# Regrouping the last output pairs, the last norm's steps, a look-ahead of weights and the low parts of the pooling in a one-core decoder step

## The chip, the cores and the metric

The kernel runs on one core of one Trainium2 chip. The time is device microseconds (us) of one launch; the kernel before takes 2322.99 us, the median of three runs (2320.79 to 2325.85). Engines are named as in the profile: PE is TensorE (PEld its weight loads), DVE is VectorE, ACT is ScalarE, POOL is GpSimd, SP is SyncE, whose queue issues most DMAs.

## The reference

One inference step of a decoder with two layers, width 2048, in fp32. There are 1024 prompt tokens and 8 sampled tokens that each continue a sequence of their own. In outline, prompt and samples alike:

```
z = x @ w_in_a;  u, gate = z[:, :2048], z[:, 2048:]
d = mean of u over the last 2, 4, 8, 16 tokens (four groups of 512 channels) - u
d = per-group linear(d) * scale
h = layer_norm(ALPHA * x + (d * silu(gate)) @ w_out_a)          # layer A
k, v = h @ w_kv                                                  # 4 heads of 64, rotary on k
q, gate = h @ w_in_b                                             # 32 heads of 64
o = attention over the last 128 tokens, with a learned sink per head
y = layer_norm(ALPHA * h + (o * silu(gate)) @ w_out_b)          # layer B
```

The outputs are y for prompt and samples, and the new pooling states, keys and values.

## The kernel before, in words

**Stages.** The tokens are cut into two chunks, c = 0 (512 tokens) and c = 1 (512 tokens and the 8 samples, 520 columns). PHASES runs the input side of layer A (ai0, ai1), its output side (ao0, ao1), the input side of layer B with the attention (bi0, bi1) and its output side (bo0, bo1). Everything is transposed: channels lie on the partitions, tokens on the free axis.

**Products.** A 2048x2048 block is multiplied by Strassen's scheme: for each pair of 128-row output tiles `seven()` makes seven products, in the order ORDER7. Every fp32 operand is split into a high part (rounded to the format that PE multiplies) and a low part (the rest), so a product is 8 row blocks times 3 matmuls (L684 to L686): 24 matmuls of 128x128 by 256 or 260 columns. Behind a product stand its posts, which take the results out of PSUM: copies on ACT (L623 p0, L632 and L657 p5 and p6, L629, L638, L644, L647) and additions on DVE (L645, L650; L636 and L655 in the last pairs).

**Weights ahead.** `begin()` (L531) runs ahead of each product. With `self.ahead = a, b, d` it issues the loads (L285, 512 KB each, on the SP queue) up to a products ahead, the high parts (L505, ACT) up to b ahead and the low parts (L520, DVE) up to d ahead. The value is 7, 4, 3 in Strassen stages, and 6, 4, 3 from the end of bi1 until 23 products into bo0. In bi1 it falls to at most 6, 3, 2 whenever fewer than three whole buffers are free. Inputs of a product (high and low part of combined x tiles, L828 loads, L838 ACT, L847 DVE) are made ahead in the same way by `x_tick`.

**Memory and order.** There are 54 buffers of 128 x 1040 floats; the one that has been free longest is taken. PE, DVE and ACT run in the order of the source (`in_order`). The SP queue issues in order too: a load whose buffer is still in use holds back everything behind it.

**From bi0 to bi1.** The last two pairs of bi0 make queries and gates of chunk 0, `queries(p)` (L2148) calls `x_begin(nxt)` at the last one, and bi1 begins with the shared keys and values: weights `in_wkv`, and input sums of h (`h1`, `th1`). Between them run the attention of chunk 0 (L1874 scores, L1923 and L1910 exponentials, L1936, L1963 store of o by POOL) and rotary's partner rows, fetched by four DMAs (L1728).

**Pooling in ai0 and ai1.** For each tile `pool_tail` (L1106) finishes the mean (L1131 subtracts u); a step later `rest()` makes the high part on ACT; `low()` makes the low part on DVE (L1150) and frees the buffers. With c = 1 low() follows at once, with c = 0 another step later.

**Norm of chunk 0 during bo1.** `ln_gen` (L1066 on) yields between steps; `end()` (L544), at the end of each product, takes a step when self.every (2.75 in bo1) products have passed and enough buffers are free. For a pair it loads the raw output (L994), subtracts the mean (L1068), multiplies by 1/sigma (L1069), applies gain and bias on ACT (L1060) and stores (L1061).

**The end, phase_end.** bo1's chunk is cut into columns A (the first 260, prompt tokens) and Bh (260 more). The last pairs, SPLIT = 5, 6, 7, called x, y, z, make their 21 products in turns, in the order TAIL; `steps` says which helper runs ahead of which product: x_in (load of the residual), less (ALPHA*h minus a shift), rest (adds the residual), square (ACT), add (accumulates sums and squares, DVE), stats (mean and 1/sigma of Bh), affine1 (L1474, L1478: subtract mean, multiply, DVE), affine2 (ACT L1485 twice, and the out_y store L1486), back (reloads an earlier pair), scale (gain, ACT) and spare (POOL). After the last product stand the last square and sums, `moments` (L1545, mean and 1/sigma of A), POOL's four steps on the last four columns (L1619 to L1622), `last_rows` (L1594: rank-one matmuls that finish the transposed rows of A) and `evict` (L1602), which scales 8 PSUM banks of 128x512 into four tiles, each stored to y1a with one DMA of 512 KB.

Of the kernel before, what the change touches and what calls it, by code (L numbers as in the profile page):

```python
# [66 lines left out]
SPLIT = 5, 6, 7  # L67
TAIL = (
    (5, 0), (5, 2), (5, 1), (6, 0), (5, 3), (5, 4), (6, 2), (6, 1), (7, 0), (6, 3), (7, 2), (7, 1), (6, 4),
    (7, 3), (7, 4), (5, 5), (5, 6), (6, 5), (6, 6), (7, 5), (7, 6),  # L70
# [120 lines left out]
class Kern:  # L191
# [789 lines left out]
    def ln_gen(self, c, pre, acc, gc, bc, out, td):  # L981
# [81 lines left out]
        for p in range(10):  # L1063
            load(p + 2)
            if p < 8:
                t = self.pair_view(pre[p], T)  # L1066
                if c == 0:
                    nc.vector.tensor_sub(t, t, b2(mu))  # L1068
                nc.vector.tensor_mul(t, t, b2(rr))  # L1069
# [52 lines left out]
    def pool_tail(self, c, i, g, w, U, s, T, ext, dd, bufs, Us, work, add):  # L1122
# [20 lines left out]
        def rest():  # L1143
# [10 lines left out]
            low() if c else self.at(1, low)  # L1154
# [249 lines left out]
    def phase_end(self, c, xs, x_in, pre, acc, gc, bc, out):  # L1404
# [30 lines left out]

        def square(p, h, j=slice(0, 2)):
            if p not in q:
                q[p] = self.mem.full(2 * T)
            nc.scalar.activation(self.pair_view(q[p], T)[:, j, h], tv(p)[:, j, h], AF.Square)

        def add(p, h):
            nc.vector.tensor_add(av[:, :, h], av[:, :, h], tv(p)[:, :, h])
            nc.vector.tensor_add(qv[:, :, h], qv[:, :, h], self.pair_view(q[p], T)[:, :, h])

        def sums(h):
# [3 lines left out]
            for ps, a, w in zip(R[h.start], (av, qv), (tv(z), self.pair_view(q[z], T))):  # L1449
                srcs = [v[:, j, h] for v in (a, w) for j in range(2)]  # L1450
# [3 lines left out]
        def stats(h):  # L1454
# [4 lines left out]
            nc.scalar.copy(m, mb[:, :TH])  # L1459
            nc.vector.tensor_mul(qq, m, m)  # L1460
# [76 lines left out]
        def sums_z(n):  # L1537

            w = (tv(z), self.pair_view(q[z], T))[n]
            for j in range(2):  # L1540
                nc.tensor.matmul(
                    R[0][n][:, :TH], J, w[:, j, A], start=False, stop=j == 1, skip_group_check=True,
                )

        def moments():  # L1545
# [15 lines left out]
            affine1a(1, Bh)  # L1561
# [7 lines left out]
            affine1b(1, Bh)  # L1569
# [32 lines left out]
        def evict(b, k):  # L1602
# [3 lines left out]
            r = box["rc"][:, b : b + 1]  # L1606
            if k % 2:
                nc.vector.tensor_scalar(y, X[b, k][:], r, None, op0=ALU.mult)  # L1608
# [3 lines left out]
            else:  # L1612
                nc.scalar.activation(y, X[b, k][:], AF.Copy, scale=r)
# [13 lines left out]
        x, y, z = SPLIT  # L1627
        for p in SPLIT:
            box, z0, z1 = self.two(T)

            def open_(p=p, box=box, z0=z0):
# [6 lines left out]
            (x, 0): [lambda: x_in(y)],  # L1638
            (x, 2): [lambda: less(x)],
            (y, 0): [lambda: x_in(z)],  # L1640
# [8 lines left out]
            (z, 3): [lambda: rest(y, Bh), lambda: square(y, Bh), lambda: back(1), lambda: back(2)],  # L1649
            (z, 4): [  # L1650
                lambda: add(y, Bh), lambda: rest(y, A), lambda: back(3), lambda: back(4),
                lambda: spare(0), lambda: scale(0),
            ],
# [13 lines left out]
        }  # L1667
        for p, idx in TAIL:
            for go in steps.get((p, idx), []):
                self.at(0, go)  # L1670
            if (p, idx) == (x, 5):
# [13 lines left out]
        scale(y)  # L1685
        spare(y)
        spare(z)
        affine1(z, Bh)
# [793 lines left out]
```

## Time and profile before

| | |
|---|---|
| Runs | 2322.99 us median, 2320.79 to 2325.85 |
| Profiled execution | 2320.17 us, span 2317.9 us (2.27 us lie outside the span) |
| Granted TensorE clock, mean | 0.997 |
| PE busy | 2288.1 us, 99% of the span |
| DVE busy | 1943.0 us, 84% |
| ACT busy | 1389.3 us, 60% |
| POOL busy | 191.1 us, 8% |
| DMA | 649.37 MB, mean 280 GB/s |
| Largest stall of PE inside the program | 4.92 us, at 1506.68 to 1511.60 us |
| Last matmul product ends | 2296.1 us after the start of the span |

Times inside the trace count from the start of the span. A row of the list of instructions gives the start, the time from start to end, engine, line, operation, output and inputs, a count, and in brackets how long the engine had been idle before it and what ended that. Rows of SPq are DMA issues. A row of the waits gives total us, times, and the longest one. A matmul is shown 0.28 us long although the next begins 0.12 us later, since they are pipelined.

### The profile page before, as it was taken

What the parts mean: (1) busy time and instruction counts of PE and PEld (TensorE: products, weight loads), DVE (VectorE), ACT (ScalarE), POOL (GpSimd) and SP (SyncE); (2) the same over time, 40 slices, a digit from 0 to 9 for tenths busy, and PEclk for the clock granted to TensorE, in tenths of its full rate; (3) what the DMA queues carried; (4) which work ended last, traced back from release to release, by engine and by line L of the source; (5) the groups of instructions that cost most, each with busy time, mean ns of one, the idle gap of its engine ahead of it and who ended that gap; (6) DMA issues with size and microseconds to landing.
All of it is one profiled execution on the core that took longest, in us unless ns stands there. A gap on an engine that the chain in (4) does not pass through costs nothing. (4 is left out here: it accounts for less than half of the span.)

```text
span 2317.9 us, 50529 instructions
## 1 busy us (share of the span) xinstructions
PE 2288.1 (99%) x20417; PEld 2217.7 (96%) x20417; DVE 1943.0 (84%) x2409; ACT 1389.3 (60%) x2548; POOL 191.1 (8%) x360
## 2 busy tenths in 40 slices
PE   9999999999999999999999999999999999999997
PEld 7999999999999999999889999989999999999997
DVE  8888889877878878988979898889877777889797
ACT  5544446544546547655566767685776678556565
POOL 0111110010000000000001111100000000000001
PEclk9999999999999999999999999999999999999999
DMA  7869679999989989999767666777787878799795
GB/s 261 287 242 315 229 245 330 315 309 303 304 302 322 335 284 333 317 392 345 245 234 241 233 234 236 252 259 250 234 252 240 252 230 288 251 360 381 252 330 184
DMA packets 246682, 649.37 MB, mean 280 GB/s; under 512 B 25232, under 2 KB 106032, under 8 KB 246448
## 3 DMA queue, kind: packets, MB, share of 16 engines
q1 hardware_dynamic: 204432, 493.66, 63.8%
q0 software_dynamic: 42016, 152.49, 17.0%
q8 instruction: 159, 2.61, 0.5%
q14 instruction: 75, 0.61, 0.1%
HBM read 463.54 MB, written 173.01 MB: 275 GB/s over the span
## 5 line engine op out<-in xcount | busy, mean ns | idle before, releaser
L684 PE MATMUL pD<-m,m 128*128 128x260 f32 (+1 forms) x5088 | 1441.3, 283 | 4.7 <-ACT pD L623 2.3
L686 PE MATMUL pD<-m,m 128*128 128x260 f32 (+1 forms) x5088 | 1434.7, 282 | 4.9 <-DVE m L520 4.9
L685 PE MATMUL pD<-m,m 128*128 128x260 f32 (+1 forms) x5088 | 1434.7, 282 | 0.0
L684 PEld LDWEIGHTS pD<-m,m 128*128 128x128 f32 x5088 | 959.4, 189 | 13.9 <-issue 6.2
L686 PEld LDWEIGHTS pD<-m,m 128*128 128x128 f32 x5088 | 959.8, 189 | 7.1 <-DVE m L520 7.0
L685 PEld LDWEIGHTS pD<-m,m 128*128 128x128 f32 x5088 | 959.1, 189 | 0.5
L520 DVE TENSOR_TENSOR m<-m,m 128x1024 fp32r<-128x1024 f32 x690 | 833.5, 1218 | 94.7 <-ACT m L505 44.1
L505 ACT CAST m<-m 128x1024 fp32r<-128x1024 f32 x690 | 720.5, 1049 | 249.9 <-DVE m L349 120.3
L349 DVE TENSOR_TENSOR m<-m,m 128x1024 f32<-128x1024 f32 x136 | 166.1, 1222 | 10.2 <-DMA m<-in_wia 5.7
L847 DVE TENSOR_TENSOR m<-m,m 128x1024 fp32r<-128x1024 f32 (+1 forms) x118 | 143.8, 1224 | 7.4 <-ACT m L838 5.8
L838 ACT CAST m<-m 128x1024 fp32r<-128x1024 f32 (+1 forms) x118 | 123.3, 1051 | 11.8 <-DVE m L520 3.5
L657 ACT COPY m<-pD 128x260 f32<-128x260 f32 (+1 forms) x89 | 33.2, 373 | 131.0 <-PE pD L686 131.0
L645 DVE TENSOR_TENSOR m<-pD,m 128x260 f32<-128x260 f32 (+1 forms) x92 | 38.4, 418 | 73.1 <-ACT pD L644 67.2
L1910 ACT ACTIVATE m<-m,sm 128x128 f32<-128x128 f32 x256 | 99.4, 392 | 0.0
L623 ACT ACTIVATE pD<-pD 128x260 f32<-128x260 f32 (+1 forms) x90 | 33.3, 370 | 102.2 <-PE pD L686 102.0
L1179 PE MATMUL pD<-m,m 128*128 128x260 f32 (+1 forms) x528 | 91.5, 323 | 0.0
L712 PE MATMUL pD<-m,m 128*128 128x512 f32 x224 | 89.1, 398 | 0.0
L714 PE MATMUL pD<-m,m 128*128 128x512 f32 x224 | 88.2, 394 | 0.0
L713 PE MATMUL pD<-m,m 128*128 128x512 f32 x224 | 88.1, 393 | 0.0
L1179 PEld LDWEIGHTS pD<-m,m 128*128 128x128 f32 x528 | 79.4, 188 | 8.2
L1923 ACT ACTIVATE m<-m,sm 128x128 f32<-128x128 f32 x256 | 81.8, 391 | 3.8 <-DVE sm L1918 3.4
L632 ACT COPY m<-pD 128x260 f32<-128x260 f32 (+1 forms) x92 | 34.3, 373 | 82.3 <-PE pD L686 82.0
(257 smaller groups left out, 2101.3 us busy)
## 6 DMA issues: line engine op xcount, KB each, us to landing
m<-in_wib SPq DMA_DIRECT2D x132, 512.0 KB
m<-in_wia SPq DMA_DIRECT2D x128, 512.0 KB
m<-swoa SPq DMA_DIRECT2D x64, 512.0 KB
swia<-m POOLq DMA_DIRECT2D x56, 512.0 KB, 4.9
m<-swia SPq DMA_DIRECT2D x56, 512.0 KB
m<-swob SPq DMA_DIRECT2D x56, 512.0 KB
m<-in_wob SPq DMA_DIRECT2D x52, 512.0 KB
m<-in_woa SPq DMA_DIRECT2D x48, 512.0 KB
```

Of the source, the lines that this page charges most:

```text
L349: self.nc.vector.tensor_add(s[out].a[:, :1024], s[x].a[:, :1024], s[y].a[:, :1024])
L505: self.nc.scalar.copy(hi.r[:, :1024], self.stream[self.cast].src().a[:, :1024])
L520: self.nc.vector.tensor_sub(lo.r[:, :1024], s.src().a[:, :1024], hi.a[:, :1024])
L684: nc.tensor.matmul(ps[:, :TH], wh[:, s], h, start=new and k == 0, stop=False, skip_group_check=on)
L685: nc.tensor.matmul(ps[:, :TH], wh[:, s], l, start=False, stop=False, skip_group_check=on)
L686: nc.tensor.matmul(ps[:, :TH], wl[:, s], h, start=False, stop=k == 7, skip_group_check=on)
L712: nc.tensor.matmul(ps[:], wh[:, s], h, start=par == 0 and k == 0, stop=False)
L714: nc.tensor.matmul(ps[:], wl[:, s], h, start=False, stop=par == 1 and k == 7)
L838: self.nc.scalar.copy(h.r[:, :n], s.a[:, :n])
L847: self.nc.vector.tensor_sub(l.r[:, :n], s.a[:, :n], h.a[:, :n])
L1179: nc.tensor.matmul(ps[:, : cs.stop - cs.start], ws[:, s], d[:, cs], start=f0 and k == 0, stop=l0 and k == 3,)
L1910: nc.scalar.activation(x["s3"][:, i, :], x["s3"][:, i, :], AF.Exp, bias=nm[:, i : i + 1], scale=0.125, accum_out=rs[:, i : i + 1],)
```

## The change

Four edits.

1. **The end.** SPLIT becomes 4, 5, 6, 7, called w, x, y, z: four pairs are made in turns, 28 products, with pair 4's last two products near the end. Squares take a half buffer each and free it in add. Every affine1 but that of y and z moves ahead of the last product, and so does affine2 of pairs 0, w, 1, 2 and x; pair 3 alone gets its affine2 later. Pair 4 needs no store and reload. Of the scale and spare steps, those of y move ahead of the last product. The evictions no longer alternate with affines, and five of the eight run on DVE, three on ACT (before, four and four).
2. **The norm of chunk 0 in bo1.** A yield stands between subtraction and multiplication when the result is the final output, and self.every falls from 2.75 to 1.5.
3. **Pooling.** low() follows at once for means over 8 and 16 tokens, and a step later for those over 2 and 4, in both chunks. So chunk 0's wide groups make it earlier, chunk 1's narrow ones later.
4. **bi0 to bi1.** From the last query pair of bi0, loads run 8 products ahead instead of 7, for 30 products: the 14 left of bi0 and 16 of bi1.

```diff
-SPLIT = 5, 6, 7
+SPLIT = 4, 5, 6, 7
...
                 if c == 0:
                     nc.vector.tensor_sub(t, t, b2(mu))
+                    if td is None:
+                        yield
                 nc.vector.tensor_mul(t, t, b2(rr))
...
-            low() if c else self.at(1, low)
+            low() if w > 4 else self.at(1, low)
...
-                q[p] = self.mem.full(2 * T)
+                q[p, h.start] = self.mem.half(T)
...
+            q.pop((p, h.start)).free()
...
             nc.scalar.copy(m, mb[:, :TH])
+            rest(z, A)
             nc.vector.tensor_mul(qq, m, m)
...
-            affine1a(1, Bh)
+            affine1a(z, Bh)
...
-            (x, 6): [
-                lambda: stats(Bh), lambda: spare(1), lambda: scale(1), lambda: spare(2), lambda: scale(2),
-            ],
-            (y, 5): [
-                lambda: square(x, A), lambda: affine(0, Bh), lambda: spare(3), lambda: scale(3),
-            ],
-            (y, 6): [
-                lambda: add(x, A), lambda: rest(z, A), lambda: spare(x), lambda: scale(x),
-            ],
-            (z, 5): [lambda: square(y, A), lambda: affine(x, Bh), lambda: spare(4), lambda: scale(4)],
+            (w, 6): [lambda: stats(Bh), lambda: spare(1), lambda: scale(1)],
+            (x, 5): [lambda: square(w, A), lambda: affine(0, Bh), lambda: spare(2), lambda: scale(2)],
+            (x, 6): [lambda: add(w, A), lambda: spare(w), lambda: scale(w)],
+            (y, 5): [lambda: square(x, A), lambda: affine(w, Bh), lambda: spare(3), lambda: scale(3)],
+            (y, 6): [lambda: add(x, A), lambda: affine(1, Bh), lambda: spare(x), lambda: scale(x)],
+            (z, 5): [lambda: square(y, A), lambda: affine(2, Bh), lambda: affine1(x, Bh)],
             (z, 6): [
-                lambda: square(z, A, 0), lambda: add(y, A), lambda: scale(z, (0,), True),
+                lambda: square(z, A, 0), lambda: add(y, A), lambda: scale(z, (0,), True), lambda: scale(y),
+                lambda: spare(y), lambda: affine1(3, Bh), lambda: affine2(x, Bh),
             ],
...
         affine1(y, Bh)
         scale(z, (1,))
-        scale(y)
-        spare(y)
         spare(z)
-        affine1(z, Bh)
...
-            affine2(z, Bh)
+            affine2(3, Bh)
         last_rows(0, range(4))
         last_rows(1, range(3))
-        affine1(2, Bh)
-        for k in range(4):
-            evict(0, k)
-        last_four()
-        affine2(1, Bh)
+        evict(0, 0, False)
+        evict(0, 1, True)
+        evict(0, 2, True)
+        affine2(z, Bh)
         X[1, 3] = self.psD()
         turn(1, 12, 16)
         last_rows(1, (3,))
-        affine1(3, Bh)
-        affine2(2, Bh)
-        for k in range(4):
-            evict(1, k)
-        affine1(4, Bh)
-        affine2(3, Bh)
-        affine2(4, Bh)
+        evict(0, 3, True)
+        last_four()
+        evict(1, 0, False)
+        evict(1, 1, True)
+        evict(1, 2, False)
+        evict(1, 3, True)
...
                 if c == 1:
                     self.ahead = 6, 4, 3
+                else:
+                    self.ahead = 8, 4, 3
+                    self.at(30, lambda: setattr(self, "ahead", (7, 4, 3)))
...
-                self.every, self.room = 2.75, 3
+                self.every, self.room = 1.5, 3
```

The SP queue at the turn from bi0 to bi1, before (in_wkv is the weight of keys and values, h and th the inputs of bi1's sums, L1728 the partner rows):

```order
L285 DMA m_1974_17956<-in_wib 128x1024
L828 DMA m_1979_18002<-h_95 128x4x260
L828 DMA m_1989_18088<-th_92 128x4x260
L1728 DMA m_1977_17995<-m_1962_17784 32x1024 x4
L828 DMA m_1978_18000<-h_95 128x4x260
L285 DMA m_1980_18006<-in_wkv 128x1024
L828 DMA m_1983_18044<-h_95 128x4x260
L828 DMA m_1984_18046<-h_95 128x4x260
L285 DMA m_1986_18050<-in_wkv 128x1024
L285 DMA m_1990_18091<-in_wkv 128x1024
```

The same place with the change (L1732 is the old L1728):

```order
L285 DMA m_1975_17958<-in_wkv 128x1024
L285 DMA m_1970_17912<-in_wib 128x1024
L828 DMA m_1979_18002<-h_95 128x4x260
L1732 DMA m_1978_17997<-m_1963_17786 32x1024 x4
L828 DMA m_1980_18004<-h_95 128x4x260
L285 DMA m_1981_18008<-in_wkv 128x1024
L828 DMA m_1984_18046<-h_95 128x4x260
L828 DMA m_1985_18048<-h_95 128x4x260
L285 DMA m_1987_18052<-in_wkv 128x1024
L828 DMA m_1990_18090<-th_92 128x4x260
```

The first load of in_wkv moves ahead of the inputs and of the partner rows, the second comes directly behind the partner rows and one input, and the load of th that stood ahead of the partner rows now stands behind the third load of in_wkv.

DVE around the end of the last product, before: L636 and L655 take z's last two products from PSUM, and then come four affines of two rows each before L1557, the first row of `moments`.

```order
L1442 TENSOR_TENSOR m_2839_26557<-m_2839_26557,m_3008_27968 128x2x260
L1443 TENSOR_TENSOR m_2921_27166<-m_2921_27166,m_3045_28331 128x2x260
L655 TENSOR_TENSOR m_3025_28141<-pD_28576,m_3025_28141 128x260
L1474 TENSOR_TENSOR m_3008_27968<-m_3008_27968,m_3058_28452 128x2x260
L1478 TENSOR_TENSOR m_3008_27968<-m_3008_27968,m_3058_28452 128x2x260
L1474 TENSOR_TENSOR m_3025_28141<-m_3025_28141,m_3058_28452 128x2x260
L1478 TENSOR_TENSOR m_3025_28141<-m_3025_28141,m_3058_28452 128x2x260
L1557 TENSOR_TENSOR m_3067_28650<-m_3066_28649 128x260
```

With the change (L1447, L1448 are the old L1442, L1443; L1481, L1485 the old L1474, L1478; L1564 the old L1557):

```order
L636 TENSOR_TENSOR m_3022_28091<-pD_28561,m_3022_28091 128x260
L1447 TENSOR_TENSOR m_2842_26560<-m_2842_26560,m_3004_27917 128x2x260
L1448 TENSOR_TENSOR m_2926_27183<-m_2926_27183,m_3048_28320 128x2x260
L1481 TENSOR_TENSOR m_3047_28313<-m_3047_28313,m_3055_28395 128x2x260
L1485 TENSOR_TENSOR m_3047_28313<-m_3047_28313,m_3055_28395 128x2x260
L655 TENSOR_TENSOR m_3022_28091<-pD_28595,m_3022_28091 128x260
L1481 TENSOR_TENSOR m_3004_27917<-m_3004_27917,m_3055_28395 128x2x260
L1485 TENSOR_TENSOR m_3004_27917<-m_3004_27917,m_3055_28395 128x2x260
L1564 TENSOR_TENSOR m_3069_28672<-m_3065_28620 128x260
```

One affine less stands between L655 and the moments, and one more ahead of L655.

The last stores of the SP queue, before (y1c are the four last columns, y1a the rows of A, out_y the columns Bh of a pair):

```order
L1623 DMA out_y1c<-area 128x64
L1609 DMA out_y1a<-m_3068_28701 128x1024
L1609 DMA out_y1a<-m_3069_28705 128x1024
L1486 DMA out_y<-m_3046_28333 128x2x260
L1486 DMA out_y<-m_3047_28335 128x2x260
L1609 DMA out_y1a<-m_3070_28728 128x1024
L1609 DMA out_y1a<-m_3071_28732 128x1024
L1486 DMA out_y<-m_3051_28372 128x2x260
L1486 DMA out_y<-m_3052_28374 128x2x260
```

With the change (L1631 the old L1623, L1493 the old L1486, L1619 the old L1609):

```order
L1631 DMA out_y1c<-area 128x64
L1493 DMA out_y<-m_3047_28313 128x2x260
L1619 DMA out_y1a<-m_3071_28722 128x1024
L1493 DMA out_y<-m_3022_28091 128x2x260
L1619 DMA out_y1a<-m_3072_28726 128x1024
L1619 DMA out_y1a<-m_3073_28744 128x1024
L1619 DMA out_y1a<-m_3074_28748 128x1024
```

Two stores of out_y (260 KB each) fewer stand behind y1c, and the last one is a store of y1a.

More of the change, by code (lines that the diff above doesn't have):

```diff
@@ L1434, in rest, with qh @@
             nc.vector.tensor_add(tv(p)[:, :, h], tv(p)[:, :, h], x[:, :, h])
+        def qh(p, h):
+            return q[p, h.start].a[:, : 2 * TH].rearrange("p (k t) -> p k t", k=2)
         def square(p, h, j=slice(0, 2)):
[L1437 to L1439 removed]
+            if (p, h.start) not in q:
+                q[p, h.start] = self.mem.half(T)
+            nc.scalar.activation(qh(p, h)[:, j], tv(p)[:, j, h], AF.Square)
         def add(p, h):
             nc.vector.tensor_add(av[:, :, h], av[:, :, h], tv(p)[:, :, h])
[L1443 removed]
+            nc.vector.tensor_add(qv[:, :, h], qv[:, :, h], qh(p, h))
+            q.pop((p, h.start)).free()
         def sums(h):
@@ L1448, in sums @@
             z = SPLIT[-1]
-            for ps, a, w in zip(R[h.start], (av, qv), (tv(z), self.pair_view(q[z], T))):
-                srcs = [v[:, j, h] for v in (a, w) for j in range(2)]
+            for ps, a, w in zip(R[h.start], (av, qv), (tv(z)[:, :, h], qh(z, h))):
+                srcs = [v[:, j] for v in (a[:, :, h], w) for j in range(2)]
                 for i, v in enumerate(srcs):
@@ L1600, in last_rows, with evict @@
                 )
-        def evict(b, k):
+        def evict(b, k, dve):
             if k % 2 == 0:
@@ L1606, in evict @@
             r = box["rc"][:, b : b + 1]
+            if dve:
+                nc.vector.tensor_scalar(y, X[b, k][:], r, None, op0=ALU.mult)
+            else:
+                nc.scalar.activation(y, X[b, k][:], AF.Copy, scale=r)
             if k % 2:
-                nc.vector.tensor_scalar(y, X[b, k][:], r, None, op0=ALU.mult)
                 nc.sync.dma_start(
@@ L1637, in phase_end @@
         steps = {
-            (x, 0): [lambda: x_in(y)],
-            (x, 2): [lambda: less(x)],
-            (y, 0): [lambda: x_in(z)],
+            (w, 0): [lambda: x_in(x)],
+            (w, 2): [lambda: less(w)],
+            (w, 4): [lambda: less(x), lambda: x_in(y)],
+            (x, 2): [lambda: rest(w, Bh)],
+            (x, 1): [lambda: square(w, Bh)],
+            (y, 0): [lambda: add(w, Bh)],
+            (x, 3): [lambda: rest(w, A), lambda: x_in(z)],
             (x, 4): [lambda: less(y)],
```

21 lines of the change are left out of this document (10 added, 11 removed).

## The prediction

> **What bounds the kernel now.** I read first the page's busy times, then what PE waited for, summed over the span, since an engine that is busy all the time gains only where it stands still.
>
> ```profile
> PE 2288.1 (99%) x20417; PEld 2217.7 (96%) x20417; DVE 1943.0 (84%) x2409; ACT 1389.3 (60%) x2548; POOL 191.1 (8%) x360
> ```
>
> ```profile
> PE pD L686 <- DVE m L520: 4.9, 9, 0.9
> PE pD L672 <- ACT m L657: 4.9, 1, 4.9
> PE pD L684 <- ACT pD L623: 2.3, 2, 1.3
> PE pD L684 <- ACT m L657: 1.6, 1, 1.6
> PE pD L1596 <- POOL area L1622: 1.3, 1, 1.3
> PE pD L684 <- ACT m L632: 0.8, 1, 0.8
> ```
>
> PE is busy for 99% of the span, and the change leaves every matmul as it is; only the order of the last ones differs. So time can come from two places alone: PE's stalls, some 19 us in all, of which the rows show the six largest groups, and the stretch behind the last product, 2296.1 to 2317.9 us, where PE is no longer the bound. The one large stall is 4.9 us at L672. All the others are 1.6 us or less.
>
> **Part 4, eight ahead from bi0 into bi1.** The lists of instructions of PE, ACT and SP at the turn:
>
> ```profile
> 1506.40 0.28 PE L686 MATMUL pD<-m,m 128*128 128x256 f32 x1
> 1511.60 1.02 PE L672 MATMUL pD<-m,m 128*128 128x260 f32 x3 [4.92 <-ACT m L657]
> ```
>
> ```profile
> 1497.28 1.06 ACT L838 CAST m<-m 128x1040 fp32r<-128x1040 f32 x1 [2.66 <-DMA m<-h]
> ...
> 1504.33 1.05 ACT L505 CAST m<-m 128x1024 fp32r<-128x1024 f32 x1 [3.49 <-DVE m L1960]
> ...
> 1510.23 1.05 ACT L838 CAST m<-m 128x1040 fp32r<-128x1040 f32 x1
> 1511.17 0.37 ACT L657 COPY m<-pD 128x256 f32<-128x256 f32 x1
> ```
>
> ```profile
> 1480.71 0.38 SPq L828 DMA_DIRECT2D m<-h  x1
> 1487.73 0.38 SPq L828 DMA_DIRECT2D m<-th  x1
> 1488.20 3.11 SPq L1728 DMA_DIRECT2D m<-m  x4
> ...
> 1494.83 2.16 SPq L285 DMA_DIRECT2D m<-in_wkv  x3
> ```
>
> ```profile
> SPq L828 <- DMA o<-m: 6.4, 1, 6.4
> ```
>
> bi0's last product ends at 1506.68, and PE waits for L657, the copy of that product on ACT, until 1511.54. L657 is late because ACT is: it stood idle 3.49 us before L505 at 1504.33, and then worked without a gap for 1504.33 to 1511.17, 6.84 us. The row names a DVE instruction as releaser, but that had been done long before; L505 makes the high part of the second in_wkv tile, whose load is the first of the three issued from 1494.83. That load was late because SP stood still from 1480.71 to 1487.73, 6.4 us of it for the landing of a store of o that held the buffer of a th input; behind it came the partner rows (3.11 us to issue) and the inputs of h, of which one kept ACT waiting too (2.66 us). With the change the same weight is queued directly behind the partner rows and one input, the first one ahead of them all, and that th input behind them. If SP goes on where it stood still, at 1481.1, the partner rows (3.11 us) and an input (0.4) are through by 1484.6, and the load starts up to 10 us earlier than 1494.83; 5 are enough.
>
> Without the 3.49 us alone L657 would end at 1508.05, 1.4 us after the product: the stall is 4.92 - 3.5 = 1.4 us. If the 2.66 us go too, ACT is ready ahead of the product's end, and what is left is the copy itself, 0.37 us and its way. I take **-4.0 us** (a stall of 0.9), between -4.5 and nothing. What is late next is not PE's input:
>
> ```profile
> 1478.00:1511.60 33.60, 28.47 (x361) 27.38 (x361) 28.94 (x37) 23.07 (x52) 3.62 (x8) 0.99 0.95 326
> 1511.60:1556.00 44.40, 44.40 (x430) 43.39 (x431) 37.15 (x44) 38.93 (x87) 1.93 (x4) 0.93 0.76 266
> 1556.00:1800.00 244.00, 243.38 (x2635) 238.23 (x2638) 202.15 (x271) 154.46 (x358) 16.64 (x25) 1.00 0.75 241
> ```
>
> (Columns: stretch, its length, busy us of PE, PEld, DVE, ACT, POOL, then the granted clock, the share and GB/s of the DMA.) Behind the turn PE runs 44.40 of 44.40 us while DVE and ACT have 7 and 5 us to spare, so the time won is not given back. The eighth weight occupies one buffer more for 30 products, and from there into bi1 the steps that sum w_out_b, which wait for free buffers, fall at other places: no price in the trace, at most the 0.62 us that PE now loses in that stretch, either way some 1 us. I count nothing.
>
> [...]
>
> **Part 3, low parts.**
>
> ```profile
> 342.91 0.68 DVE L1150 TENSOR_TENSOR m<-m,m 128x512 fp32r<-128x512 f32 x1
> ...
> 353.61 1.23 DVE L847 TENSOR_TENSOR m<-m,m 128x1040 fp32r<-128x1040 f32 x1
> ```
>
> ```profile
> 410.45 0.69 DVE L1150 TENSOR_TENSOR m<-m,m 128x520 fp32r<-128x520 f32 x1
> ...
> 412.53 2.35 DVE L520 TENSOR_TENSOR m<-m,m 128x1024 fp32r<-128x1024 f32 x2
> ```
>
> The count of instructions stays. In ai0 a wide group's L1150 leaves the place at 342.9, and an input's L847 (1.23 us, now at 353.6) comes there: 1.23 - 0.68 = 0.55 us more ahead of low parts of weights for which PE waits at 350.3, one of its nine waits for L520. In ai1 a narrow group's L1150 (0.69 us) leaves the place ahead of the L520 at 412.53, for which PE waits at 413.8, the longest of the nine (0.9). +0.55 and -0.69: **0 us**, with -1.2 and +1.1 as bounds, if one of the two happens twice and the other not.
>
> **Part 2, the norm during bo1.**
>
> ```profile
> 2261.56 1.22 DVE L1068 TENSOR_TENSOR m<-m,m 128x1024 f32<-128x1024 f32 x1
> 2262.81 1.23 DVE L1069 TENSOR_TENSOR m<-m,m 128x1024 f32<-128x1024 f32 x1
> ```
>
> ```profile
> 2267.44 1.51 ACT L1060 ACTIVATE m<-m,prm 128x512 f32<-128x512 f32 x2
> 2268.86 0.35 ACT L632 COPY m<-pD 128x260 f32<-128x260 f32 x1
> ```
>
> ```profile
> 2145.00:2200.00 55.00, 55.00 (x459) 54.84 (x458) 42.94 (x47) 33.20 (x47) 2.09 (x3) 1.00 0.75 250
> 2200.00:2252.00 52.00, 52.00 (x434) 51.81 (x433) 50.76 (x49) 31.48 (x47) 1.07 (x2) 1.00 0.92 324
> ```
>
> The steps now end before the last pairs begin to turn: at 2269.27 PE no longer waits 0.80 us for L632, which the two L1060 (1.51 us) hold up. The same 16 rows of 1.22 us come earlier, in single steps of 1.2 instead of 2.4 us, into 2145 to 2200, where DVE has 12 us to spare; from 2200 to 2252, where it has only 1.2, some of them go away. **-0.8 us**, from -0.8 to +1.8 if the denser steps make PE wait twice as long for an L520 as its longest such wait (0.9).
>
> **Part 1, the end.** The stretch behind the last product, from the chain that ended last and the lists of PE, DVE and SP; and what the DMA moved from 2307.0 to 2315.7, when the last packet landed:
>
> ```profile
> 2296.13 0.43 DVE m L655
> ...
> 2299.24 0.36 DVE m L1557
> ...
> 2304.19 0.49 PE pD L1596
> ```
>
> ```profile
> 2304.85 0.70 DVE L1478 TENSOR_TENSOR m<-m,m 128x520 f32<-128x520 f32 x1
> 2305.47 1.40 DVE L1608 TENSOR_SCALAR m<-pD,sm 128x512 f32<-128x512 f32 x2
> ```
>
> ```profile
> 2306.28 0.99 SPq L1609 DMA_DIRECT2D out_y1a<-m  x2
> ...
> 2310.83 2.46 SPq L1486 DMA_DIRECT2D out_y<-m  x2
> ```
>
> ```profile
> DMA packets 1660, 3.16 MB, mean 364 GB/s; under 512 B 124, under 2 KB 1148, under 8 KB 1660
> ```
>
> ```profile
> 2276.00:2296.10 20.10, 20.10 (x155) 19.63 (x155) 15.31 (x25) 12.69 (x24) 2.63 (x5) 1.00 0.38 135
> ```
>
> Ahead of the last product, DVE had 15.31 of 20.10 us to do. In the seven products from (w, 6) on, 20.0 us, it now gets nine pairs of rows of 128x520 (affines of 0, w, 1, 2, x and 3, three adds), at 1.3 us a pair 11.7 us; four L520 at 1.13, seven additions from PSUM at 0.38, and five rows of stats, 1.8 us: 20.7 us. So DVE falls about 1.5 us behind, and L655 comes near 2297.8 instead of 2296.13. Behind it stands one affine less (1.3 us), and the chain of moments reaches L1596 some **0.5 us** later, near 2304.7. From there it is shorter: the second eviction no longer stands behind the affine that ends at 2305.55, nor any other, and the last issue of SP falls near 2309 (five evictions on DVE at 0.7) instead of 2312.1.
>
> But the DMA was full all the time: 3.16 MB at 364 GB/s, 8.7 us. Now it has four y1a of 0.524 MB and one out_y of 0.266, 2.36 MB, or 6.5 us at the same rate. With the first y1a issued as now (0.5 us later chain, one affine less ahead) the flow starts near 2307.2 and ends at 2313.7 instead of 2315.7: **-2.0 us**. Bounds: -3.2, if the last issue sets the end (2309 and the 3.6 us from 2312.1 to 2315.7 behind it); +2.0, if DVE is another product behind (2.85) and the end moves with it.
>
> **The sum.** -4.0, 0, -0.8, -2.0: -6.8 us. The profiled execution, 2320.17 us, would become 2313.4. It stands 2.82 us under the median, so on the median's scale **2316.2 us**. About 0.2%, 4.6 us, is what a measurement of this kernel can tell from no change.
>
> **Rivals.**
>
> *The queue blocks all the same.* The edit doesn't do what it says if another load, now ahead of in_wkv, waits for a buffer that a store of o still holds: SP waited 6.4 us for one such. For it: eight ahead takes its buffers earlier, when fewer are free. Against: the rows ahead of the second in_wkv use buffers that were read by PE, not stored. Then the first term is 0: 2320.2 us. Chance 0.17.
>
> *DVE is the bound at the end.* For it: 20.7 us of work in 20.0, and every low part behind it. Against: PE's next operands were made products ahead. Then L1596 moves by 2 us more and part 1 gives nothing: 2318.2, up to 2320. Chance 0.13.
>
> *Buffers run short, slower.* With one weight more in flight, an input of bi1 or bo0 waits for its buffer behind a store; the queue is in order, so all weights behind it come late. The price is the stall that the same thing made here, 4.9 us, each time; it decides as soon as the wait exceeds the lead of the weights behind, some three products (8.5 us), beside the 7.0 us that SP stood still here. Together with the first stall kept, one such place gives 2320.2 + 4.9 = 2325.1, two 2330. Against it: bi1 falls back to six ahead when fewer than three buffers are free. Chance 0.12.
>
> **How the numbers follow.** The forecast has 0.58 and by its bounds lies between 2311 and 2319. Of the rivals the first lies within 0.2% of the median, the second half in, half below, the third mostly above 2327.6. Faster by over 0.2% (under 2318.4): 0.54 + 0.06 = 0.60; slower (over 2327.6): 0.10; within: 0.30. The range 2311 to 2323 leaves out some 0.05 below and 0.13 above.
>
> **What would show it.** Right: L672 idle 0.4 to 1.5 us, no idle of 3.5 us on ACT's L505 there, SP with no wait of 6 us on a store ahead of the partner rows; no wait for L632 in bo1; L655 near 2297.8, L1596 near 2304.7 (both less about 5 us for what was won before), and 6 to 7 us of full DMA behind. Wrong: a stall of over 3 us at L672, new waits of PE for L520 between 2100 and 2290 of more than 1.5 us in all, or a stretch from the last product to the end that isn't shorter than 21.8 us.

## The result, and the profile after

The changed kernel takes **2311.45 us** (median of 6 runs, 2309.76 to 2313.14), the kernel before, beside it, 2323.14. The ratio is 0.9951, 95% interval 0.9938 to 0.9964: 11.7 us less, between 8 and 14. Forecast were 2316.2 and a range of 2311 to 2323: the sign was right, the size was not, 6.9 us against 11.7. The profiled execution took 2312.54 us, with a span of 2309.7, and PE is busy for 2287.9 us (before 2288.1). The spans of that pair of executions differ by 8.2 us; why not by 11.7 is said under "The median".

What PE waited for, in the trace after (us in all, times, the longest; L1603 is the old L1596, L1630 the old L1622):

```profile
PE pD L686 <- DVE m L520: 4.6, 6, 2.1
PE pD L684 <- ACT pD L623: 2.3, 2, 1.3
PE pD L684 <- ACT m L657: 2.0, 1, 2.0
PE pD L730 <- DVE m L2205: 1.3, 1, 1.3
PE pD L1603 <- POOL area L1630: 1.3, 1, 1.3
PE pS L1878 <- DVE m L1848: 0.5, 1, 0.5
PE pD L672 <- ACT m L657: 0.5, 1, 0.5
PE pO L1955 <- DVE m L1941: 0.4, 1, 0.4
PE pD L684 <- ACT m L632: 0.4, 1, 0.4
```

The 4.9 us at L672 have become 0.5, and the 0.8 for L632 0.4. The longest wait for L520 has grown from 0.9 to 2.1, and the one for L657 behind bi1 from 1.6 to 2.0. The row of L730 is the start of the program, 1.3 us before the change too. How much later or earlier PE reaches the same matmul says more than the waits alone:

| The same matmul of PE | before, us | after, us | after - before |
|---|---|---|---|
| ai1, behind the wait at 413.8 | 413.80 | 414.71 | +0.9 |
| L672, first of bi1 | 1511.60 | 1508.19 | -3.4 |
| in bi1's first product | 1516.96 | 1511.27 | -5.7 |
| in bo0's first product | 1955.31 | 1951.96 | -3.4 |
| first behind the last product | 2295.93 | 2291.20 | -4.7 |
| first last-row matmul | 2304.19 | 2299.45 | -4.7 |
| end of the span | 2317.9 | 2309.7 | -8.2 |

**The turn from bi0 to bi1.** PE, SP and ACT after:

```profile
1507.44 0.28 PE L686 MATMUL pD<-m,m 128*128 128x256 f32 x1
1508.19 0.62 PE L672 MATMUL pD<-m,m 128*128 128x260 f32 x3 [0.46 <-ACT m L657]
```

```profile
1482.00 0.38 SPq L828 DMA_DIRECT2D m<-h  x1
1484.04 3.60 SPq L1732 DMA_DIRECT2D m<-m  x4
1487.74 0.52 SPq L828 DMA_DIRECT2D m<-h  x1
1488.37 0.62 SPq L285 DMA_DIRECT2D m<-in_wkv  x1
```

```profile
1500.37 1.05 ACT L505 CAST m<-m 128x1024 fp32r<-128x1024 f32 x1 [1.01 <-DVE m L520]
...
1507.76 0.37 ACT L657 COPY m<-pD 128x256 f32<-128x256 f32 x1 [0.44 <-PE pD L686]
```

```profile
SPq L828 <- DVE m L895: 4.6, 1, 4.6
```

Ahead of the partner rows SP no longer waits for a store; its wait there is 4.6 us, for DVE, ahead of the input at 1482.00. The second in_wkv load starts at 1488.37 instead of 1494.83, ACT is ready before PE, and L657 waits for PE. Then the clock (stretch, length, PE, PEld, DVE, ACT, POOL, granted clock, DMA), in the trace before and after:

```profile
1511.60:1517.40 5.80, 5.80 (x27) 5.80 (x27) 3.28 (x3) 4.57 (x12) 0.00 (x0) 0.50 1.05 389
```

```profile
1508.19:1511.60 3.41, 3.41 (x27) 3.38 (x28) 3.34 (x5) 3.41 (x10) 0.00 (x0) 1.00 1.02 384
```

The same 27 matmuls took 5.80 us at half the clock before and 3.41 us now: another 2.4 us.

**The end.** PE, DVE and SP behind the last product, and the DMA from 2301.5 to 2307.6:

```profile
2291.20 1.92 PE L1540 MATMUL pD<-m,jr 128*128 128x260 f32 x8
2292.95 1.92 PE L1548 MATMUL pD<-m,jr 128*128 128x260 f32 x8
...
2299.45 1.16 PE L1603 MATMUL pD<-m,m 128*128 128x512 f32 x4 [1.31 <-POOL area L1630]
```

```profile
2292.72 0.42 DVE L655 TENSOR_TENSOR m<-pD,m 128x260 f32<-128x260 f32 x1
...
2294.43 0.43 DVE L1564 TENSOR_TENSOR m<-m 128x260 f32<-128x260 f32 x1
```

```profile
2301.08 0.34 SPq L1619 DMA_DIRECT2D out_y1a<-m  x1
2301.72 0.37 SPq L1493 DMA_DIRECT2D out_y<-m  x1
2302.36 2.35 SPq L1619 DMA_DIRECT2D out_y1a<-m  x3
```

```profile
DMA packets 800, 2.23 MB, mean 366 GB/s; under 512 B 64, under 2 KB 320, under 8 KB 800
```

L655 comes 1.52 us behind the product instead of 0.20, as forecast, but the moments begin 3.23 us behind it, as before (3.31): PE's eight sums of the other pairs (L1540, 1.75 us to the next) stand between, and L1548 is no later. From the first last-row matmul to the end of the span are 10.2 us instead of 13.7.

### The profile page after: what moved, and what is told of

The parts are those of the page before. It is cut to its first block, busy times and chain, and to the rows that moved or that the text cites. A ratio compares the mean times of both kernels' runs of the same rounds, so it can differ in the third digit from the quotient of the medians.

```text
span 2309.7 us, 50532 instructions
## 1 busy us (share of the span) xinstructions
PE 2287.9 (99%) x20417; PEld 2217.7 (96%) x20417; DVE 1943.9 (84%) x2415; ACT 1389.2 (60%) x2547; POOL 191.1 (8%) x359
## 4 chain that ended last, share of the span: by engine, by line
PE 55%; DVE 2%; DMA 1%; ACT 0%; issue 0%; POOL 0%; DVEq 0%; POOLq 0%; SPq 0%
PE pD L684 14%; PE pD L686 14%; PE pD L685 14%; PE pO L1955 2%; PE pD L712 2%; PE pD L713 2%; PE pD L714 2%; PE pS L1878 2%; PE pS L1931 1%; PE pS L1955 0%; DMA m<-swob 0%; DVE m L520 0%; DMA m<-in_wob 0%; PE pO L684 0%; PE pO L686 0%
## 5 line engine op out<-in xcount | busy, mean ns | idle before, releaser
L684 PE MATMUL pD<-m,m 128*128 128x260 f32 (+1 forms) x5088 | 1441.0, 283 | 4.6 <-ACT pD L623 2.3
L684 PEld LDWEIGHTS pD<-m,m 128*128 128x128 f32 x5088 | 959.0, 188 | 13.8 <-issue 6.2
L520 DVE TENSOR_TENSOR m<-m,m 128x1024 fp32r<-128x1024 f32 x690 | 834.4, 1219 | 97.0 <-ACT m L505 40.7
L349 DVE TENSOR_TENSOR m<-m,m 128x1024 f32<-128x1024 f32 x136 | 166.2, 1222 | 10.1 <-DMA m<-in_wia 6.9
L847 DVE TENSOR_TENSOR m<-m,m 128x1024 fp32r<-128x1024 f32 (+1 forms) x118 | 143.9, 1225 | 7.1 <-ACT m L838 5.5
L657 ACT COPY m<-pD 128x260 f32<-128x260 f32 (+1 forms) x88 | 32.9, 373 | 122.9 <-PE pD L686 122.9
L632 ACT COPY m<-pD 128x260 f32<-128x260 f32 (+1 forms) x92 | 34.4, 374 | 78.6 <-PE pD L686 78.4
```

Source lines behind the costliest of these rows:

```text
L349: self.nc.vector.tensor_add(s[out].a[:, :1024], s[x].a[:, :1024], s[y].a[:, :1024])
L520: self.nc.vector.tensor_sub(lo.r[:, :1024], s.src().a[:, :1024], hi.a[:, :1024])
L684: nc.tensor.matmul(ps[:, :TH], wh[:, s], h, start=new and k == 0, stop=False, skip_group_check=on)
L847: self.nc.vector.tensor_sub(l.r[:, :n], s.a[:, :n], h.a[:, :n])
```

## The experiments

Theory after the result: the stall at L672 cost its idle time and, behind it, the clock, in all 7 us; the end gains by fewer bytes in a full queue; the other two edits are worth a microsecond or less. The rivals: only idle time counts and the clock's fall has another cause; the stores' issue sets the end; the low parts or the norm bring the rest. Each kernel was timed beside the kernel before on the same chip.

| Kernel | median, us | before, us | ratio (95%) |
|---|---|---|---|
| look-ahead of 8 alone | 2314.38 | 2322.32 | 0.9970 (0.9960 to 0.9981) |
| low parts alone | 2319.32 | 2322.32 | 0.9989 (0.9980 to 0.9998) |
| norm alone | 2320.85 | 2322.32 | 0.9994 (0.9985 to 1.0003) |
| before, 36 matmuls in the stall | 2318.74 | 2322.32 | 0.9986 (0.9978 to 0.9995) |
| end and norm | 2318.15 | 2323.63 | 0.9979 (0.9970 to 0.9989) |
| changed, without low parts | 2309.09 | 2323.63 | 0.9939 (0.9927 to 0.9952) |
| changed, matmuls ahead of bo0 | 2310.63 | 2323.63 | 0.9943 (0.9931 to 0.9956) |
| changed, half of the last stores | 2308.49 | 2323.63 | 0.9935 (0.9920 to 0.9950) |
| changed, again | 2311.34 | 2322.98 | 0.9955 (0.9942 to 0.9967) |
| changed, low parts in chunk 1 only | 2310.73 | 2322.98 | 0.9950 (0.9936 to 0.9964) |
| the last, with matmuls ahead of bo0 | 2309.06 | 2322.98 | 0.9946 (0.9934 to 0.9959) |
| before, 18 matmuls in the stall | 2319.83 | 2322.98 | 0.9991 (0.9981 to 1.0002) |

### The look-ahead alone

```diff
                 if c == 1:
                     self.ahead = 6, 4, 3
+                else:
+                    self.ahead = 8, 4, 3
+                    self.at(30, lambda: setattr(self, "ahead", (7, 4, 3)))
```

> The kernel before with the look-ahead of 8 alone. Theory (the stall's price is its idle time and the half-speed clock behind it): L672's idle falls from 4.92 to about 0.5 us and the first product of bi1 takes 2.9 us instead of 5.3, so PE is some 6.9 us earlier at 1517 us of before; if the 2.3 us that the changed kernel gave back between 1517 and 1955 belong to this edit, the end is 4.6 us earlier, 2318.5 us on the median's scale, and PE's stall before bo0's first product is near 1.95 us with a slow clock behind it; if they belong to other edits or to chance, 6.9 us, 2316.2. Rival (only the idle time counts, as predicted): 4.0 to 4.5 us at 1517.

```profile
1508.39 0.63 PE L672 MATMUL pD<-m,m 128*128 128x260 f32 x3 [0.46 <-ACT m L657]
```

The idle time is 0.46 us, and PE goes from 1.2 us late ahead of the turn to 5.5 early in bi1's first product: 6.7 us, the theory's number, not the rival's 4.0 to 4.5. Some of it is lost again: PE is 4.8 us early at 2264. The ratio, 7 us (4 to 9), is larger than the pair of profiles gives.

### The clock by itself

```diff
                 h = xs[0][0].rv(4, TH)[:, 0, :]
+                if self.ph == "bi1":
+                    o = self.pso.tile([P, 512], F32, tag="O", name=self.nm("pO"))
+                    for _ in range(36):
+                        nc.tensor.matmul(o[:, :256], w[0].r[:, :P], w[0].r[:, P:384], start=True, stop=True)
```

> The kernel before with 36 additional matmuls of 128x256 (their results are never read) ahead of L672, so that PE works through most of the 4.92 us in which it waited, 36 x 0.118 = 4.2 us; nothing else is changed and L657 ends when it did. Theory (the granted clock falls because PE stood still): the first product of bi1 takes 2.9 us instead of 5.3 and PE is 2.5 us earlier at 1520, 2320.6 us at the end, with L657 ending at 1511.5 as before. Rival (the clock falls there for another reason, as the DMA's load, or the slow product is no cost): no gain, or 0.3 us later.

PE, ACT and the clock in the kernel before with the 36 matmuls (L673; L676 is the old L672):

```profile
1506.59 4.48 PE L673 MATMUL pO<-m 128*128 128x256 f32 x36
1511.68 0.63 PE L676 MATMUL pD<-m,m 128*128 128x260 f32 x3 [0.61 <-ACT m L657]
```

```profile
1511.26 0.36 ACT L657 COPY m<-pD 128x256 f32<-128x256 f32 x1
```

```profile
1511.60:1517.40 5.80, 5.72 (x47) 5.70 (x48) 3.40 (x3) 5.77 (x16) 0.00 (x0) 1.00 1.06 391
```

L676 starts when it did (1511.68, before 1511.60), yet the clock stays at 1.00 and PE is 2.4 us earlier at the end of that product. With the same DMA load (391 GB/s, before 389) and L657 as late (1511.26, before 1511.17), only PE's standing still was taken away. The time falls by 3.3 us (1 to 5). That the fall of the clock follows the idle time is shown; the rival falls.

The same with 18 matmuls:

```diff
-                    for _ in range(36):
+                    for _ in range(18):
```

> The kernel before with 18 instead of 36 additional matmuls ahead of L672: PE works 2.1 us more and still stands still for 2.8 us. Theory (standing still for about 2 us or more lets the clock fall in most cases, as 1.95 to 2.16 us did in four traces): the first product of bi1 takes 4.3 to 5.3 us. [...]

PE in that kernel:

```profile
1508.59 2.31 PE L673 MATMUL pO<-m 128*128 128x256 f32 x18
1513.46 0.62 PE L676 MATMUL pD<-m,m 128*128 128x260 f32 x3 [2.55 <-ACT m L657]
...
1514.49 0.28 PE L689 MATMUL pD<-m,m 128*128 128x260 f32 x1
...
1514.97 0.42 PE L689 MATMUL pD<-m,m 128*128 128x260 f32 x1
```

After 2.55 us of idle time the matmuls go at full rate for 1.1 us, and then for 3.4 us at half (0.42 us long, 0.22 apart). A matmul of the second product that comes 5.87 us behind L676 with 36 matmuls comes 7.39 us behind it here, and 8.38 in the kernel before. So 2.55 us of standing still were enough here and cost 1.5 us of clock; 4.92 us cost 2.5.

### Each of the other edits alone

```diff
                     nc.vector.tensor_sub(t, t, b2(mu))
+                    if td is None:
+                        yield
...
-                self.every, self.room = 2.75, 3
+                self.every, self.room = 1.5, 3
```

> The kernel before with the norm's edit in bo1 alone. Theory: PE's wait of 0.80 us for L632 at 2269 goes or falls to 0.4, the 0.66 us at 2030 go, so 1 to 1.4 us less, 2321.9 us. Rival (the denser steps cost as much as they save): within 0.3 us of before. The end behind the last product is as before, 21.8 us.

From 1960 us of before, behind the slow clock at bo0, to the last product PE gains 1.1 us on the trace before: the wait of 0.8 for L632 goes, one for L520 at 2097 grows from 0.9 to 1.4. That is the theory's number, at its lower end; the ratio's interval holds 1, so the times don't show it.

```diff
-            low() if c else self.at(1, low)
+            low() if w > 4 else self.at(1, low)
```

> The kernel before with the low parts' edit alone. Theory: PE's stall at 350 us grows from 0.75 to about 2.1 us, that at 413.8 disappears (0.94) and that at 404 stays near 0.3; PE is 0.9 us later at 420 us, 2324.0 us at the end. Rival (as predicted, 0): both shift by about half a microsecond and cancel.

Here the theory was wrong. The wait at 350 us is 2.1 us and PE is 0.75 us late behind 413.8, as expected, but the kernel is faster, by 2.6 us (0.5 to 4.6). SP, ACT and PE at the turn, some 1000 us after the last instruction that was moved:

```profile
1483.16 2.01 SPq L828 DMA_DIRECT2D m<-h  x2
1485.26 3.67 SPq L1728 DMA_DIRECT2D m<-m  x4
...
1494.87 0.34 SPq L285 DMA_DIRECT2D m<-in_wkv  x1
```

```profile
1503.80 1.05 ACT L505 CAST m<-m 128x1024 fp32r<-128x1024 f32 x1 [2.71 <-DVE m L847]
...
1510.66 0.36 ACT L657 COPY m<-pD 128x256 f32<-128x256 f32 x1
```

```profile
SPq L285 <- DMA m<-h: 4.3, 2, 3.3
```

```profile
1511.08 0.63 PE L672 MATMUL pD<-m,m 128*128 128x260 f32 x3 [2.30 <-ACT m L657]
```

SP doesn't wait for the store of o. low() frees buffers, and buffers are handed out in the order in which they came free, so it can give later loads other ones; that this is the reason is argued, not tried. It isn't what makes the kernel faster: the second in_wkv load waits 3.3 us for a load of h instead and is issued at 1494.87, before at 1494.83, and L657 starts only 0.5 us earlier (1510.66, before 1511.17). But PE reaches the turn 2.1 us later than before, so it stands still for 2.30 us instead of 4.92, and no slow clock follows (the next matmuls are 0.12 us apart, as at full rate). Behind the turn it is 3.0 us early: 0.5 by ACT, 2.5 by the clock. What PE had lost until then was taken out of a wait that it had anyway.

```diff
-            low() if w > 4 else self.at(1, low)
+            low() if c else self.at(1, low)
```

> The changed kernel without the low parts' edit. Theory (what is lost in ai0 is carried to the end, since nothing behind it waits for a fixed time any more): PE waits 0.75 us instead of 2.11 at 350 us and 0.94 more at 413.8, it is 0.5 to 0.9 us earlier at 420 us, and the end 0.5 to 0.9 earlier, 2310.7. Rival (the loads at the turn from bi0 to bi1 fix the time there, as in the kernel before, where the edit alone made L672's stall 2.3 instead of 4.9): the stall before bi1 grows by what was won, and the end is the same or later.

PE waits less than 0.7 us at 350 instead of 2.1, and is 1.4 us earlier than in the changed kernel at 413, 1.5 at 1452 and 2.3 at 1945: nothing is lost on the way, and the rival falls. The times' intervals overlap, so that it is faster is seen in the traces, not in the times.

```diff
-            low() if w > 4 else self.at(1, low)
+            low() if c and w > 4 else self.at(1, low)
```

> The changed kernel with the half of the low parts' edit that seemed to pay: chunk 0 as in the kernel before (low parts a step later for all means), chunk 1 as in the changed one. Theory (chunk 0's earlier low parts cost 1.4 us, chunk 1's later ones win 0.9, and both reach the end): PE waits 0.75 us at 350 us and not at all at 413.8, and the end is 1.4 us before that of the changed kernel. Rival (lost again further on): the same time within 0.5 us.

PE is 1.2 us earlier than the changed kernel at 405, but 0.7 at 1019 and 0.3 at 1938, and the end 0.7 us earlier: half of what was expected.

### The end

The change's diff without two of its hunks:

```diff
-            low() if w > 4 else self.at(1, low)
+            low() if c else self.at(1, low)
...
-                else:
-                    self.ahead = 8, 4, 3
-                    self.at(30, lambda: setattr(self, "ahead", (7, 4, 3)))
```

> The kernel before with the end's edit and the norm's, without the look-ahead of 8 and without the low parts' edit. Theory (the parts as the two traces have them): L672's stall of 4.9 us and the slow clock behind it as before; 1 to 1.4 us less in bo1; the first row of the moments comes 3.3 us after the last product as before, although the addition from PSUM comes 1.5 us after it instead of 0.2, since PE's eight sums of the other pairs (1.75 us) stand between; from the first last-row matmul to the span's end 10.2 us instead of 13.7. In all 4.7 us, 2317.6. Rival (as predicted): the moments 0.5 us later and the stores 2.5 us shorter, 2.0 in the end and 0.8 in bo1, 2319.5.

From the first last-row matmul to the end 10.26 us, the moments 3.24 us behind the last product: the theory's numbers, and the time is 4.9 us less (2.6 to 7.0), not 2.8. But L672 waits only 2.2 us here, because PE was 3.4 us late ahead of it (1.8 us of waiting for rotary at 1501, and behind that a stretch of half clock from 1502.93, 1.5 us); so the profile has another sum than the theory.

```diff
-                    io["y1a"][b * P : (b + 1) * P, (k - 1) * 512 : (k + 1) * 512], Y[b, k // 2].a[:, :1024]
+                    io["y1a"][b * P : (b + 1) * P, (k - 1) * 512 : k * 512], Y[b, k // 2].a[:, :512]
```

> The changed kernel whose last four stores to y1a write only the first half of their columns (the other half of y1a is left out), with as many DMAs at the same times. Theory (the DMA's rate sets the end): 1.05 MB fewer at 366 GB/s, so the stretch from the first last-row matmul to the span's end is 7.5 to 7.9 us instead of 10.2, and the time 2.5 us less, 2309.0. Rival (the last issue and what lies behind a store set it): the smaller last store saves its own 0.7 us at most, 9.5 us.

From the first last-row matmul to the end 8.4 us instead of 10.2, the last packet 6.5 us behind it instead of 8.5. That is 2.0 us of the 2.9 that 1.05 MB take at 366 GB/s (the expectation had 2.5), and more than the rival's 0.7: the bytes set most of the end, and with half of them in the last stores the issue comes into sight.

### Towards a faster kernel

The changed kernel, unaltered:

> The changed kernel once more, beside the next two on the same chip: 2311.5 us within 1.5, a wait of about 2.1 us of PE at 350 us, and 10.2 us from the first last-row matmul to the span's end.

It took 2311.34 us; the wait at 350 us was 1.9 us, and the end took 10.2.

```diff
             ps = B[bank]
+            if self.warm:
+                self.warm = False
+                f = self.pso.tile([P, 512], F32, tag="O", name=self.nm("pO"))
+                for _ in range(14):
+                    nc.tensor.matmul(f[:, :256], w[0].r[:, :P], w[0].r[:, P:384], start=True, stop=True)
...
+            self.warm = (kind, c) == ("bo", 0)
```

> The changed kernel with 14 additional matmuls of 128x256 (1.65 us, their results are never read) ahead of bo0's first product, where PE stands still for 1.5 to 2.0 us. Theory (near 2 us of standing still the granted clock falls for the next 5 us in some executions): the idle time there falls under 0.5 us and the first product takes 3.0 us instead of 4.3, 1.3 us earlier in executions that fell, 0 in the others, so 0 to 1.3 us in the median. Rival (the matmuls delay the product, or the clock falls anyway): no gain or up to 1.6 us later.

In the trace after, the clock in bo0's first product had fallen, which it hadn't before (1.00 from 1952.50 to 1956.00); with the matmuls it stays (1943.00 to 1949.50):

```profile
1947.70:1953.10 5.40, 5.40 (x33) 5.40 (x34) 5.33 (x7) 5.31 (x14) 0.00 (x0) 0.68 1.05 383
```

```profile
1943.00:1949.50 6.50, 6.46 (x56) 6.26 (x54) 6.40 (x8) 6.47 (x19) 0.00 (x0) 1.00 1.06 390
```

PE is 1.6 us earlier than in the trace after at 1453, 3.5 at 1959 and 3.6 at the last product. Its time beside the kernel before (0.9943) is not clear of the changed kernel's (0.9951 and, again, 0.9955).

The same matmuls and the low parts in chunk 1 only, together:

> The same, with the 14 additional matmuls ahead of bo0's first product, so that PE stands still for less than 0.7 us there. Theory: another 0 to 1.3 us less than with the low parts alone, 2309 us and less spread between executions, 2 to 2.7 us before the changed kernel. Rival: no better than either edit alone.

It has the lowest median of its session, 2309.06 beside 2311.34, but the intervals overlap. In its trace the clock holds at bo0 (1.00 from 1944 to 1950), and what was won, 3.0 us at 2084, is lost again at one place, 1.7 us by a longer wait and 1.5 by half clock behind it:

```profile
PE pD L691 <- DVE m L520: 6.0, 8, 2.7
```

```profile
2089.68:2093.09 3.41, 3.41 (x18) 3.41 (x18) 3.32 (x4) 2.80 (x5) 0.53 (x1) 0.50 1.05 406
```

The wait of 2.7 us ends at 2088.35. The changed kernel waits there 0.96 us until 2089.68, run again 2.13 until 2088.26, and with low parts in chunk 1 only 3.06 until 2088.86: PE comes earlier and goes on at nearly the same time. Run again, the changed kernel has half clock behind this wait too (1.5 us; the mean from 2089 to 2145 is 0.97); behind the 3.06 us the clock stays (1.00 over the same 56 us). In the last of these, SP's waits from 2060 to 2092 have

```profile
SPq L285 <- DMA to<-m: 4.7, 1, 4.7
```

a weight behind a buffer whose store has to land: SP's wait of the old stall, at another place. The changed kernels with matmuls ahead of bo0 alone and without low parts went on there at 2086.2 and 2086.3, so the time is not fixed in all; the cause was not tried.

## Why the prediction was right or wrong

**The turn: right in mechanism, too small by the clock.** Cause, queue and idle time came as forecast: -4.46 us of idle against -4.0. The step that failed is the price of the stall: "the stall is 4.92 - 3.5 = 1.4 us" takes the idle time for all of it. Behind it stood 2.3 us more of half clock (6.7 us in all from 1506 to 1517), which 36 matmuls alone took away. It could have been read: the row 1511.60 to 1556.00 that the prediction shows has 0.93 in the clock's column, where all its neighbours have 1.00 or 0.99; 7% of 44.4 us is 3.1 us. The clock fell behind 4.92 us, but also behind 1.95 to 2.16 us in four traces, and not behind 2.11 (trace after, at 350), 2.30 and 3.06: the length of a stall alone didn't tell here.

Two waits, with end and norm alone (1.81 us) and with low parts in chunk 1 only (3.06 us, until 2088.86):

```profile
1499.52:1502.93 3.41, 1.60 (x68) 1.35 (x68) 3.34 (x6) 3.41 (x5) 0.29 (x1) 1.00 1.06 386
1502.93:1506.34 3.41, 3.41 (x19) 3.41 (x18) 3.41 (x5) 1.49 (x4) 0.05 (x2) 0.50 1.03 403
```

```profile
2083.66:2087.07 3.41, 2.14 (x19) 1.94 (x17) 2.07 (x5) 0.00 (x0) 0.13 (x1) 1.00 1.03 381
2087.07:2090.49 3.42, 1.63 (x13) 1.63 (x14) 3.42 (x4) 1.51 (x2) 0.41 (x1) 1.00 1.04 406
```

Behind the first the clock is 0.50 from 1502.93 on; around the second, the longer one, it stays at 1.00. So of these two waits the shorter one cost clock and the longer one didn't; what decides was not shown.

**"The time won is not given back": wrong.** Of the 5.7 us at 1517 2.3 were gone at 1955, most of them where bo0 begins: the stall there grew from 1.62 to 1.95 us, and the clock fell behind it (0.50 from 1948.71 to 1952.12), 1.5 us. In the changed kernel run again that stall was 1.46 us, shorter than before: the chance of an execution, not a cost of eight ahead that could be shown.

**Low parts: 0 forecast, +0.9 measured at 414 us.** The gain at 413.8 came (0.9), the loss at 350.3 was 1.4 us, not 0.55: beside the longer L847, the weight's L349 ahead of it had to wait longer for its load and began at 343.27 instead of 341.77. Four more executions with the edit in chunk 0 waited 1.9 to 2.1 us there, and in them PE's wait of 1.3 us for ACT that follows in the others (L684, at 354) was gone. The larger effect was not in the sum at all: alone, the edit makes PE come later to the turn and so keeps the clock. With eight ahead hardly a wait is left there (0.46 us), so the gain is missing and the loss is not hidden, as the changed kernel without the edit shows.

**The norm: right.** -0.8 forecast; -0.8 from 2030 to the last product in the trace after, and -1.0 over the same stretch alone.

**The end: right in direction, -2.0 forecast, -3.5 measured.** The sum had +0.5 us for a later chain of moments; DVE was late by the forecast 1.5 us, but this stands beside PE's sums and costs nothing. The first y1a is issued 1.6 us behind the first last-row matmul instead of 2.1, and the rate (366 GB/s, forecast 364) then gives what was said. The last 0.4 us lie behind the last packet: 1.7 us to the end of the span, where the last store is y1a, instead of 2.2. Of its bounds, the -3.2 is -3.1 by its own numbers (2309 + 3.6 against 2315.7), and the measured -3.5 lies outside.

**The median.** The profiled execution of before was 3 us under its median, and the sum was moved up by that without asking what it lacked. Of five other executions with the old end, four have 14.6 to 15.0 us from the first last-row matmul instead of 13.7 (one 13.8), while seven with the new one have 10.2 to 10.3: the end is worth 3.5 us in the first pair and 4.4 by the medians. Four executions without eight ahead were idle for 2.0 to 2.2 us ahead of bo0 and had a slow clock of 1.6 us there, which the profiled one, at 1.62 us of idle, escaped. With 6.7 for the turn, 4.4 for the end and 0.8 for the norm the sum is 11.9, beside 11.7 measured; that the loss in ai0 and what bo0 gives back are made up by such slow clocks in other executions of before is argued, not shown.

**The range: in part luck.** The four best bounds together, -4.5, -1.2 (twice 0.69 would be -1.4), -0.8 and -3.2, give 2313.3 on the median's scale, and the worst 2327.9; "by its bounds" 2311 to 2319 doesn't follow. The measured 2311.45 lies below that 2313.3. It is inside the range of 2311 to 2323 because the range was drawn wider than its rows.

The rivals: SP never waited for a store at the turn, DVE did not bound the end, and no load of bi1 came late. That a load behind a store stops PE may have come true later, at 2088, where gains are lost; one trace shows SP waiting so there, and no run tries it.

## What to carry to other kernels

Price a stall of TensorE with the clock behind it: read the granted clock in the few microseconds after each long idle stretch, and if it falls, the stall costs the idle time and, here, another 1.5 us for 3.4 us of half clock; where the wait itself can't be removed, matmuls without a use may keep the clock: here 36 of them, which left 0.61 us of idle time, did (1.00), and 18, which left 2.55 us, didn't. Where a queue issues in order and buffers go round, ask for each load on the path what stands ahead of it and whose store must land first; an edit a thousand microseconds earlier changed here which load waited. Where an edit elsewhere shortens a stall, see first whether the engine only came later to it: time lost ahead of a wait whose end another engine sets costs nothing, and time won there gains nothing until that wait is gone. At the end of a program sum the bytes that are still to be stored and divide by the rate before counting instructions: work that ran beside a full queue, or beside matmuls that had to run anyway, cost nothing here (DVE's last addition came 1.52 us behind the product instead of 0.20, the moments 3.23 instead of 3.31).

## What the runs showed of the hardware

- PE's clock fell to half behind waits of 4.92 us (before: 0.50 from 1510.64 to 1517.47, 6.83 us), 2.7 (low parts in chunk 1 only, with matmuls ahead of bo0: 0.50 from 2089.68 to 2093.09), 2.55 (18 matmuls in the stall: matmuls 0.22 us apart for 3.4 us, from 1.1 us after PE had gone on), 1.95 (after: 0.50 from 1948.71 to 1952.12, 3.41 us) and 1.81 (end and norm: 0.50 from 1502.93 to 1506.34, from 1.6 us after PE had gone on). It did not fall behind 3.06 us (low parts in chunk 1 only: 1.00 from 2083.66 to 2090.49 and from 2089 to 2145), 2.30 (low parts alone: the next matmuls 0.12 us apart), 2.11 (after, at 350: 1.00 from 350 to 370) and 1.62 (before, at 1951: 1.00 from 1950 to 1960).
- From the last packet to the end of the span were 2.2 us (profile before) where the last stores are tiles of 128x2x260, 2.9 in the look-ahead alone with the same stores, and 1.7 us where the last store is a tile of 128x1024.
- The changed kernel's DMA moved 384 GB/s over the 56 us from 2089 to 2145 (last number):

```profile
2089.00:2145.00 56.00, 55.21 (x461) 55.00 (x462) 52.40 (x50) 41.83 (x56) 1.59 (x3) 1.00 1.03 384
```
